# Half of the later feed-forward output pieces get their low part from an adding transfer, and the residual stands in DRAM while it is summed

## The chip, the cores and the metric

One core of a Trainium2 chip runs one decoder layer in float32. Five engines work side by side, each from its own list of instructions in order: TensorE (PE) multiplies, VectorE (DVE) and ScalarE (ACT) do elementwise work, GpSimd (POOL) does a little of that and issues transfers, and SyncE (SP) issues transfers. Instructions wait for each other by semaphores. The metric is the device time of one execution in microseconds (us).

## What is computed

A post-norm layer over 256 tokens of 2048 values: a feed-forward half step, a mixer (sparse attention beside a linear recurrence, with gates), and a second feed-forward half step, each added to its scaled input and normalised.

```python
def swiglu(h, w_in, w_out):
    a, b = jnp.split(h @ w_in, 2, axis=-1)
    return (jax.nn.silu(a) * b) @ w_out

h = layer_norm(DN_ALPHA * h + 0.5 * swiglu(h, ffn1_w_in, ffn1_w_out), ln1_g, ln1_b)
...                                     # mixer, merged
h = layer_norm(DN_ALPHA * h + merged @ w_out, ln2_g, ln2_b)
h = layer_norm(DN_ALPHA * h + 0.5 * swiglu(h, ffn2_w_in, ffn2_w_out), ln3_g, ln3_b)
```

D_FF is 5632, so each feed-forward reads an input matrix of 2048 x 11264 and an output matrix of 5632 x 2048. The change touches the two feed-forwards alone.

## The kernel before

**Three products for one.** PE multiplies in a rounded float32 form. To keep precision, each weight and each activation is split into a high part (the value rounded to that form) and a low part (the rest). A product is then three matmuls (`three`, L638 to L641): activation high by weight high, activation high by weight low, activation low by weight high.

**Pieces.** All weights come in the order of one list, `pieces`, each 128 x 1024 values (512 KB) or a part of a chunk of 128 x 2048 (1 MB). `Weights.load_to` has SP load piece i + 8 into a buffer `raw` (4 of these) or, for chunks, `rf` (2 of these) when PE's program is at piece i. `Weights.split_to` makes the two parts of piece i + 4: ScalarE copies with rounding into `wh` (L229), VectorE subtracts and writes `wl` (L230); there are 5 buffers of each. `unit` hands the parts to the matmuls.

**Chunks and plain pieces.** In a feed-forward the 22 column blocks of the input matrix follow each other. A block takes its weights as plain pieces (two products of 512 columns by two token tiles, 12 matmuls in all) or as chunks in a form with seven half-size products in place of eight (4 pieces named p1q3, p2, q5p7, q4p6; 12, 6, 12 and 12 matmuls of 256 columns), for which VectorE makes sums of weights first (L192, L196, L199). From block 6 on a block has four output pieces (`"o"` in its plan) and two plain input pieces beside three chunks (18 pieces), or four chunks and no plain input piece (20 pieces).

**The output product.** The 5632 rows of the output matrix are cut into six segments. While a segment's successor is being computed, output pieces of the segment run between its input pieces: `fill` multiplies one piece (12 matmuls of 512 columns) and after the last of four ScalarE takes the sums out of PSUM with a factor of 0.5 into `yd` (L1050), and POOL issues a transfer that adds `yd` to the residual `Y` in SBUF (L1051). Eight tiles `Y` of 128 x 512 hold the residual; they are among the 53 buffers of 128 x 512 that `U` hands out. The last segment has no successor: its pieces come after block 21, and its sums are added to `Y` by VectorE (`y_add`, L772), which then feeds the norm.

**What sets the order.** PE, SP and POOL run in the order in which the program writes their instructions. ScalarE's and VectorE's order is made by a scheduler from priorities and dependencies. Small tasks (norms, residual, gates) are stepped in the background once a piece.

## Time and profile before

| | |
|---|---|
| three runs | 2378.07, 2378.59, 2378.8 us (median 2378.59) |
| the profiled execution | 2379.03 us, its span 2377.3 us |
| PE busy | 2360.8 us (99%) |
| VectorE busy | 2211.1 us (93%) |
| ScalarE busy | 1491.2 us (63%) |
| DMA, loads by SP / transfers by POOL | 54.9% / 8.1% of 16 engines' span |
| clock granted to PE | 1.0 throughout |

How to read it: a row of a group gives line, engine, operation, tiles, shapes and count, then busy time and the mean of one in ns, then the idle time before it and what ended that. A row of waits gives who waited for whom, the sum in us, how often, and the longest. A row of the order of time gives start and duration in us. The span begins with the first instruction; the 1.7 us between span and time lie around it.

### The profile page before, as it was taken

To read this page: it belongs to the slowest core of one execution; us is meant where nothing else is said; L and a number is where in the kernel's file an instruction comes from. 1 tells how busy PE (TensorE), PEld (TensorE's weight loads), DVE (VectorE), ACT (ScalarE), POOL (GpSimd) and SP (SyncE) were. 2 spreads that over 40 slices of the span, in tenths; PEclk is the share of its full clock that TensorE was granted. 3 is DMA by queue.
4 is the path that set the end of the run, shared out by engine and by line. 5 is a ranking of instruction groups with operands and counts; after the bars stand their busy time and mean duration, and the time that the engine had idled before them with its cause. 6 is when DMAs were issued, how large, how long until landed. Compare 5 with 4: busy or idle time off the path is not lost.

```text
span 2377.3 us, 38831 instructions
## 1 busy us (share of the span) xinstructions
PE 2360.8 (99%) x14926; PEld 2106.8 (89%) x14926; DVE 2211.1 (93%) x3130; ACT 1491.2 (63%) x2040; POOL 123.8 (5%) x196
## 2 busy tenths in 40 slices
PE   9999999999999999999999999999999999999999
PEld 7898999989988888888999998888898899899997
DVE  7999999999999998789878889998999999999997
ACT  7666666666647555665578886555766666666663
POOL 0000000000000000001000001100000000000000
PEclk9999999999999999999999999999999999999999
DMA  8666666666566455537655558755676665676665
GB/s 302 192 226 211 223 213 221 218 218 213 189 219 222 177 186 172 191 132 269 208 185 183 182 181 292 263 199 173 208 231 213 222 212 187 230 230 210 215 214 177
DMA packets 123163, 499.69 MB, mean 210 GB/s; under 512 B 14272, under 2 KB 15552, under 8 KB 102112
## 3 DMA queue, kind: packets, MB, share of 16 engines
q1 hardware_dynamic: 104400, 453.03, 54.9%
q0 software_dynamic: 18576, 44.17, 8.1%
q8 instruction: 117, 1.92, 0.3%
q14 instruction: 70, 0.57, 0.1%
HBM read 465.68 MB, written 10.49 MB: 200 GB/s over the span
## 4 chain that ended last, share of the span: by engine, by line
PE 93%; DVE 4%; issue 1%; DMA 1%; ACT 0%; SPq 0%; POOL 0%; POOLq 0%; ACTq 0%; DVEq 0%
PE mm L641 20%; PE mm L639 20%; PE mm L640 20%; PE bp L640 6%; PE bp L641 6%; PE bp L639 6%; PE mm L1337 3%; PE mm L1339 3%; PE mm L1338 3%; DVE wl L230 2%; PE bp L1029 1%; DVE ws L192 0%; DMA x<-x_fm 0%; DMA raw<-f1a 0%; ACT wh L229 0%
## 5 line engine op out<-in xcount | busy, mean ns | idle before, releaser
L229 ACT ACTIVATE wh<-raw 128x1024 fp32r<-128x1024 f32 (+2 forms) x538 | 547.2, 1039 | 286.9 <-PE mm L641 162.8
L230 DVE TENSOR_TENSOR wl<-raw,wh 128x1024 fp32r<-128x1024 f32 (+2 forms) x538 | 631.3, 1191 | 96.8 <-ACT wh L229 94.6
L229 ACT ACTIVATE wh<-rf 128x1024 fp32r<-128x1024 f32 (+1 forms) x489 | 440.0, 915 | 312.9 <-PE mm L641 153.0
L230 DVE TENSOR_TENSOR wl<-rf,wh 128x1024 fp32r<-128x1024 f32 (+1 forms) x489 | 505.5, 1040 | 11.5 <-ACT wh L229 5.9
L639 PE MATMUL mm<-wh,hs 128*128 128x512 f32 (+1 forms) x884 | 317.0, 359 | 0.0
L641 PE MATMUL mm<-wh,hs 128*128 128x512 f32 (+1 forms) x884 | 311.2, 352 | 1.2 <-DVE hs L820 1.2
L640 PE MATMUL mm<-wl,hs 128*128 128x512 f32 (+1 forms) x884 | 310.8, 352 | 0.2 <-DVE wl L230 0.2
L641 PE MATMUL mm<-wh,g 128*128 128x512 f32 (+1 forms) x696 | 274.6, 394 | 0.0
L639 PE MATMUL mm<-wh,g 128*128 128x512 f32 (+1 forms) x696 | 274.4, 394 | 0.0
L640 PE MATMUL mm<-wl,g 128*128 128x512 f32 (+1 forms) x696 | 274.4, 394 | 0.0
L229 ACT ACTIVATE wh<-ws 128x1024 fp32r<-128x1024 f32 x163 | 173.1, 1062 | 144.1 <-PE mm L641 86.0
L639 PE MATMUL bp<-wh,sh 128*128 128x256 f32 x918 | 258.7, 282 | 0.0
L640 PE MATMUL bp<-wl,sh 128*128 128x256 f32 x918 | 256.4, 279 | 1.2 <-DVE wl L230 1.2
L641 PE MATMUL bp<-wh,sl 128*128 128x256 f32 x918 | 256.2, 279 | 0.0
L192 DVE TENSOR_TENSOR ws<-rf 128x1024 f32<-128x1024 f32 x163 | 198.4, 1217 | 9.5 <-DMA rf<-wrb 2.8
L230 DVE TENSOR_TENSOR wl<-ws,wh 128x1024 fp32r<-128x1024 f32 x163 | 198.1, 1215 | 1.3 <-ACT wh L229 1.0
L641 PEld LDWEIGHTS mm<-wh,hs 128*128 128x128 f32 x884 | 165.9, 188 | 27.6 <-DVE hs L820 2.6
L639 PEld LDWEIGHTS mm<-wh,hs 128*128 128x128 f32 x884 | 166.0, 188 | 24.3 <-issue 1.5
L640 PEld LDWEIGHTS mm<-wl,hs 128*128 128x128 f32 x884 | 166.1, 188 | 22.4 <-DVE wl L230 0.7
L1337 PE MATMUL mm<-hs,wh 128*128 128x256 f32 x640 | 179.8, 281 | 0.0
L1338 PE MATMUL mm<-hs,wh 128*128 128x256 f32 x640 | 179.8, 281 | 0.0
L1339 PE MATMUL mm<-hs,wl 128*128 128x256 f32 x640 | 179.8, 281 | 0.0
(353 smaller groups left out, 5276.3 us busy)
## 6 DMA issues: line engine op xcount, KB each, us to landing
rf<-f1a SPq DMA_DIRECT2D x64, 1024.0 KB, 5.4
rf<-f2a SPq DMA_DIRECT2D x64, 1024.0 KB, 5.7
raw<-f1o SPq DMA_DIRECT2D x88, 512.0 KB, 6.6
raw<-f2o SPq DMA_DIRECT2D x88, 512.0 KB, 6.6
raw<-wB SPq DMA_DIRECT2D x80, 512.0 KB, 4.0
raw<-wG SPq DMA_DIRECT2D x54, 512.0 KB, 4.3
raw<-f2a SPq DMA_DIRECT2D x48, 512.0 KB, 4.4
raw<-f1a SPq DMA_DIRECT2D x47, 512.0 KB, 5.4
```

The costliest lines, as they stand in the source:

```text
L192: v.tensor_tensor(t, b[:, 0:4:3], b[:, 1:2].to_broadcast([P, 2, 2, 256]), op=OP.add)
L229: nc.scalar.activation(hp, src, AF.Copy)
L230: self.last = nc.vector.tensor_tensor(lp, src, hp, op=OP.subtract)
L639: T.matmul(ps, xh, w[0], start=start, stop=False)
L640: T.matmul(ps, xh, w[1], start=False, stop=False)
L641: T.matmul(ps, xl, w[0], start=False, stop=stop)
L1029: T.transpose(ps[:, k * S + t * P:k * S + (t + 1) * P], z[:, t * 512 + k * P:t * 512 + (k + 1) * P], ident)
L1337: T.matmul(ps[:, :S], w[0], x[:, 0], start=first, stop=False)
L1338: T.matmul(ps[:, :S], w[0], x[:, 1], start=False, stop=False)
L1339: T.matmul(ps[:, :S], w[1], x[:, 0], start=False, stop=last)
```

## The change

Of the four output pieces of a segment and column block, the second and the fourth (`k` 2 and 6) in segments 1 to 4 are marked: two a block in blocks 6 to 21, 32 in each feed-forward.

A marked piece leaves the usual path. `far_to` loads its raw weights 14 pieces ahead (still 512 KB by SP, into `raw`), and ten pieces ahead ScalarE writes, for each half of 512 columns, the negated rounded weights into a tile `l` and the rounded weights into a tile `h` (both `wd`, from `U`); POOL issues a transfer that reads the same weights again from DRAM and adds them to `l`. What stands in `l` then is the weight minus its rounded form, the low part. VectorE's subtraction and the wide copy of such a piece are gone, and it uses no `wh` and `wl`.

The residual also leaves SBUF: at the start of each feed-forward's sums POOL stores the scaled residual to tiles `sums` in DRAM, the adding transfers of `fill` go there, and after block 21 eight transfers load it into fresh tiles `Y`.

```diff
@@ -59,6 +59,7 @@
 WS_BUFS = 1
 HL_BUFS = 5
 AHEAD = 4
+EARLY = 10
 LOADS = 4
 FORMS = ("p1q3", "p2", "q5p7", "q4p6")
 PIECE = 1024
@@ -151,6 +152,31 @@
         self.cur = -1
         self.limit = None
         self.off = 0
+        self.far = []
+        self.far_raw = {}
+        self.far_loaded = self.far_split = 0
+
+    def far_to(self, i):
+
+
+        nc = self.nc
+        while self.far_loaded < len(self.far) and self.far[self.far_loaded] <= i + LOADS:
+            k = self.far[self.far_loaded]
+            ap = self.pieces[k][0]
+            t = self.far_raw[k] = self.pool.tile([P, PIECE], F32, name=f"raw{k}", tag="raw", bufs=RAW_BUFS)
+            nc.sync.dma_start(t, ap)
+            self.far_loaded += 1
+        while self.far_split < len(self.far) and self.far[self.far_split] <= i:
+            k = self.far[self.far_split]
+            ap, t = self.pieces[k][0], self.far_raw.pop(k)
+            h, l = ([self.wide() for _ in range(2)] for _ in range(2))
+            for c in range(2):
+                nc.scalar.activation(l[c], t[:, c * 512:(c + 1) * 512], AF.Copy, scale=-1.0)
+                nc.gpsimd.dma_start(l[c], ap[:, c * 512:(c + 1) * 512], accum_op=OP.add)
+            for c in range(2):
+                nc.scalar.activation(h[c], t[:, c * 512:(c + 1) * 512], AF.Copy)
+            self.hl[k] = (h, l)
+            self.far_split += 1
 
     def key(self, i):
         ap, form = self.pieces[i]
@@ -165,7 +191,7 @@
         while self.loaded <= min(i, len(self.pieces) - 1):
             ap, form = self.pieces[self.loaded]
             k = self.key(self.loaded)
-            if k not in self.raw:
+            if k not in self.raw and self.loaded not in self.far:
                 n = ap.shape[1]
                 if form:
                     t = self.fast_pool.tile([P, 2 * PIECE], F32, name=f"rf{self.loaded}", tag="rf", bufs=RAWF_BUFS)
@@ -205,6 +231,9 @@
         nc = self.nc
         while self.split <= min(i, len(self.pieces) - 1):
             form = self.pieces[self.split][1]
+            if self.split in self.far:
+                self.split += 1
+                continue
             self.load_to(self.split)
             k = self.key(self.split)
             if self.split >= len(self.pieces) - WIDE:
@@ -238,6 +267,7 @@
             self.hl.pop(self.cur, None)
             self.cur += 1
             self.off = 0
+            self.far_to(self.cur + EARLY)
             self.load_to(self.cur + AHEAD + LOADS)
             self.split_to(self.limit or self.cur + AHEAD)
             self.on_piece()
@@ -245,7 +275,7 @@
         o = self.off
         self.off += n
         assert self.off <= self.size(self.cur)
-        if self.cur >= len(self.pieces) - WIDE:
+        if self.cur >= len(self.pieces) - WIDE or self.cur in self.far:
             return h[o // 512], l[o // 512]
         return h[:, o:o + n], l[:, o:o + n]
 
@@ -335,7 +365,7 @@
 
     bg = Background()
 
-    pieces = []
+    pieces, far = [], []
 
     def plain(aps):
         for ap in aps:
@@ -349,6 +379,8 @@
                 pieces.append((ap[:, k * 512:k * 512 + PIECE], None))
             elif f == "o":
                 g, nb, k = next(fills)
+                if k in (2, 6) and g:
+                    far.append(len(pieces))
                 k += 2 * SEGS[g][0]
                 pieces.append((fo[nb][:, k * 512:k * 512 + PIECE], None))
             else:
@@ -395,6 +427,7 @@
     ffn_pieces(f2a, f2o)
 
     W = Weights(nc, pool, pieces, bg.step)
+    W.far = far
     W.wide = lambda: U("wd", F32R)
     W.fast_pool = ctx.enter_context(tc.tile_pool(name="f1", bufs=1))
     lane, first_home, shared = [None], {}, ExitStack()
@@ -589,6 +622,8 @@
 
     Y = [[None] * 4 for _ in range(2)]
 
+    sums = [[[spill.tile([P, 512], F32, name=name("ya")) for _ in range(4)] for _ in range(2)] for _ in range(2)]
+
     def load_x():
         for _ in range(4):
             yield
@@ -600,6 +635,7 @@
         for nb in range(4):
             for t in range(2):
                 A.activation(Y[t][nb], Y[t][nb], AF.Copy, scale=ALPHA)
+                G.dma_start(sums[0][t][nb], Y[t][nb])
                 yield
 
     bg.add("y", load_x())
@@ -609,7 +645,7 @@
         G.dma_start(t, bass.AP(tensor=v.tensor, offset=v.offset + nb * 512, ap=[[0, P], [1, 512]]))
         return t
 
-    def residual(g, b, away=None):
+    def residual(g, b, away=None, to=None):
         for nb in range(4):
             gr, br = row(g, nb, "gr"), row(b, nb, "br")
             if away:
@@ -622,6 +658,8 @@
                 V.scalar_tensor_tensor(y, y, ALPHA, gr, op0=OP.mult, op1=OP.mult)
                 yield
                 V.scalar_tensor_tensor(y, br, ALPHA, y, op0=OP.mult, op1=OP.add)
+                if to:
+                    G.dma_start(to[t][nb], y)
                 yield
 
 
@@ -1035,6 +1073,7 @@
         g = [[None] * (2 * (b1 - b0)) for b0, b1 in SEGS]
         fills = iter(FILLS)
         open_ps = []
+        acc = sums[ln.last]
 
         def fill():
             s, nb, k0 = next(fills)
@@ -1048,7 +1087,7 @@
                 for t in range(2):
                     u = W.fast_pool.tile([P, 512], F32, name=name("yd"), tag="yd", bufs=2)
                     A.activation(u, open_ps[t], AF.Copy, scale=0.5)
-                    G.dma_start(Y[t][nb], u, accum_op=OP.add)
+                    G.dma_start(acc[t][nb], u, accum_op=OP.add)
 
         for s, (b0, b1) in enumerate(SEGS):
             for n in range(b0, b1):
@@ -1057,6 +1096,10 @@
                 with tc.high_priority():
                     next(task)
                 bg.add("gate", task)
+        for nb in range(4):
+            for t in range(2):
+                Y[t][nb] = U("y")
+                G.dma_start(Y[t][nb], acc[t][nb])
         new_stats((24, 30) if ln.last else (24, 24))
         if not ln.last:
             share("t")
@@ -1437,7 +1480,7 @@
 
 
     new_stats()
-    ln = InnerNorm("ln2_g", "ln2_b", FAST, lambda: bg.add("main", residual(ln2_g, ln2_b)))
+    ln = InnerNorm("ln2_g", "ln2_b", FAST, lambda: bg.add("main", residual(ln2_g, ln2_b, None, sums[1])))
     out_product(mg, ln, mg_forms)
     mg = mg_forms = None
     share("s")
```

Three places show how the rows move; numbers in `wh`, `wl`, `raw`, `rf` are those of the piece. They are taken at the end of block 9 of the first feed-forward: piece 152 is its successor's first output piece, 153 and 165 are marked ones of block 10, 143 is a marked one of block 9.

ScalarE, before, from the last chunk of block 9 to the output pieces of block 10:

```order
L229 ACTIVATE wh146_2959<-ws144_2932 128x1024
L229 ACTIVATE wh147_2976<-rf144_2855 128x1024
L1050 ACTIVATE yd168_2992<-mm159_2779 128x512
L1050 ACTIVATE yd169_2995<-mm160_2780 128x512
L229 ACTIVATE wh148_3000<-rf148_2928 128x1024
L229 ACTIVATE wh149_3020<-rf148_2928 128x512
L229 ACTIVATE wh150_3033<-ws148_3002 128x1024
L229 ACTIVATE wh151_3052<-rf148_2928 128x1024
L229 ACTIVATE wh152_3070<-raw152_2998 128x1024
L229 ACTIVATE wh153_3086<-raw153_3018 128x1024
L229 ACTIVATE wh154_3096<-raw154_3031 128x1024
L229 ACTIVATE wh155_3112<-raw155_3050 128x1024
```

ScalarE, now, from the same chunk on (`L174` writes the tile that the transfer adds to, `L177` the rounded weights):

```order
L258 ACTIVATE wh146_3033<-ws144_3006 128x1024
L174 ACTIVATE wd218_3052<-raw153_2988 128x512
L174 ACTIVATE wd219_3053<-raw153_2988 128x512
L177 ACTIVATE wd216_3050<-raw153_2988 128x512
L177 ACTIVATE wd217_3051<-raw153_2988 128x512
L258 ACTIVATE wh147_3060<-rf144_2931 128x1024
```

After four more rows of the same list:

```order
L258 ACTIVATE wh150_3115<-ws148_3086 128x1024
L258 ACTIVATE wh151_3134<-rf148_3002 128x1024
L258 ACTIVATE wh152_3152<-raw152_3082 128x1024
L258 ACTIVATE wh154_3174<-raw154_3113 128x1024
L258 ACTIVATE wh155_3192<-raw155_3132 128x1024
L174 ACTIVATE wd229_3279<-raw165_3190 128x512
L258 ACTIVATE wh156_3221<-rf156_3150 128x1024
```

The one copy of piece 153, which stood behind wh152, has become four and stands between wh146 and wh147; the first of piece 165 stands between wh155 and wh156. In the list of now the five `wh` before wh146 belong to the pieces 145, 144, 142, 141 and 140, since 143 is a marked one.

SP, before, the loads of the same pieces:

```order
L178 DMA rf139_2750<-f1a 128x2048
L178 DMA raw143_2835<-f1o 128x1024
L178 DMA rf144_2855<-f1a 128x2048
L178 DMA rf148_2928<-f1a 128x2048
L178 DMA raw152_2998<-f1o 128x1024
L178 DMA raw153_3018<-f1o 128x1024
L178 DMA raw154_3031<-f1o 128x1024
L178 DMA raw155_3050<-f1a 128x1024
L178 DMA rf156_3068<-f1a 128x2048
L178 DMA raw160_3139<-f1a 128x1024
L178 DMA rf161_3159<-f1a 128x2048
L178 DMA raw165_3231<-f1o 128x1024
```

SP, now:

```order
L167 DMA raw143_2794<-f1o 128x1024
L204 DMA rf139_2818<-f1a 128x2048
L204 DMA rf144_2931<-f1a 128x2048
L167 DMA raw153_2988<-f1o 128x1024
L204 DMA rf148_3002<-f1a 128x2048
L204 DMA raw152_3082<-f1o 128x1024
L204 DMA raw154_3113<-f1o 128x1024
L204 DMA raw155_3132<-f1a 128x1024
L204 DMA rf156_3150<-f1a 128x2048
L167 DMA raw165_3190<-f1o 128x1024
L204 DMA raw160_3219<-f1a 128x1024
L204 DMA rf161_3239<-f1a 128x2048
```

The loads of 143, 153 and 165 stand one or two rows further ahead; none is added.

POOL, before, in the same blocks, where it issues nothing but the adding transfers into `Y`:

```order
L1051 DMA y58_398<-yd156_2702 128x512
L1051 DMA y59_400<-yd157_2705 128x512
L1051 DMA y63_429<-yd168_2992 128x512
L1051 DMA y64_431<-yd169_2995 128x512
L1051 DMA y48_336<-yd180_3394 128x512
L1051 DMA y49_338<-yd181_3397 128x512
```

POOL, now:

```order
L175 DMA wd218_3052<-f1o 128x512
L175 DMA wd219_3053<-f1o 128x512
L1090 DMA ya29_206<-yd220_3076 128x512
L1090 DMA ya33_210<-yd221_3079 128x512
L175 DMA wd229_3279<-f1o 128x512
L175 DMA wd230_3280<-f1o 128x512
L175 DMA wd238_3400<-f1o 128x512
L175 DMA wd239_3401<-f1o 128x512
```

The two transfers of piece 153 (`wd218`, `wd219`) stand ahead of the pair that adds the sums ending with piece 143, those of piece 165 (`wd229`, `wd230`) behind it.

## The prediction

> **What bounds the kernel now.** I read the page's busy shares first, then the waits of TensorE over the whole span.
>
> ```profile
> PE 2360.8 (99%) x14926; PEld 2106.8 (89%) x14926; DVE 2211.1 (93%) x3130; ACT 1491.2 (63%) x2040; POOL 123.8 (5%) x196
> PEclk9999999999999999999999999999999999999999
> ```
>
> ```profile
> PE mm L639 <- ACT wh L229: 5.6, 1, 5.6
> ...
> PE bp L640 <- DVE wl L230: 1.2, 2, 0.7
> ...
> PE mm L640 <- DVE wl L230: 0.2, 1, 0.2
> ```
>
> These are the first, the fifth and the last of eight rows, which sum to 11.6 us of 2377. Half of it is the first weight at the start. VectorE, whose work the change removes, is the cause of 1.4 us. The change acts on blocks 6 to 21 of both feed-forwards, about 140 to 661 us and 1790 to 2313 us, so I asked for the waits there: for all engines in the first stretch (130 to 661), and for PE alone in the second (1800 to 2310), where one row is the whole answer.
>
> ```profile
> ACT wh L229 <- PE mm L641: 105.8, 95, 2.2
> ...
> DVE wl L230 <- ACT wh L229: 6.1, 10, 1.0
> ```
>
> ```profile
> PE bp L640 <- DVE wl L230: 0.5, 1, 0.5
> ```
>
> In the first stretch PE itself has no wait at all (its own answer is empty), and ScalarE's largest wait is for PE to give a buffer back (106 us, 95 times): the makers of operands run ahead of PE and are held by it. The busy times by stretch (columns: PE, PEld, DVE, ACT, POOL, then granted clock, DMA share, GB/s) say how close the race is.
>
> ```profile
> 940.00:990.00 50.00, 50.00 (x238) 41.36 (x238) 37.06 (x79) 27.52 (x56) 1.90 (x4) 1.00 0.56 176
> 301.00:396.00 95.00, 95.00 (x625) 86.22 (x623) 93.13 (x111) 60.76 (x75) 5.25 (x6) 1.00 0.66 216
> 1875.00:2050.00 175.00, 175.00 (x1142) 158.54 (x1142) 172.14 (x204) 111.10 (x135) 8.96 (x11) 1.00 0.65 211
> ```
>
> VectorE is 98% busy in the blocks (93.13/95), yet PE is never idle. A busy PE is not a PE at its peak, so I took its starts from the order of time.
>
> ```profile
> 302.57 0.28 PE L639 MATMUL mm<-wh,xs 128*128 128x256 f32 x1
> 302.69 0.28 PE L640 MATMUL mm<-wl,xs 128*128 128x256 f32 x1
> 303.97 0.39 PE L639 MATMUL mm<-wh,xs 128*128 128x512 f32 x1
> 304.20 0.39 PE L640 MATMUL mm<-wl,xs 128*128 128x512 f32 x1
> ```
>
> ```profile
> 941.91 0.39 PE L640 MATMUL mm<-wl,hs 128*128 128x512 f32 x1
> 942.15 0.40 PE L641 MATMUL mm<-wh,hs 128*128 128x512 f32 x1
> ```
>
> A product of 256 columns starts about 0.117 us after the one before, one of 512 about 0.233 us, and the second pair shows the same step where VectorE is only 74% busy (37.06/50) and the DMA at 0.56. In the blocks PE's own stream sets the time; VectorE only keeps up, with 2% to spare.
>
> **The change part by part.** The sum is made against the profiled execution's own time, 2379.03 us (span 2377.3 and 1.7 around it); the three runs' median is 2378.59, 0.44 below, and the forecast is moved by that.
>
> *Work taken from VectorE and given to ScalarE.* 64 pieces (32 in each feed-forward, two in each of 16 blocks) lose one wide subtraction and one wide copy, and get four half-wide copies.
>
> ```profile
> L230 DVE TENSOR_TENSOR wl<-raw,wh 128x1024 fp32r<-128x1024 f32 x516 | 620.1, 1219 | 93.9 <-ACT wh L229 91.7
> L229 ACT ACTIVATE wh<-raw 128x1024 fp32r<-128x1024 f32 x516 | 536.9, 1061 | 281.3 <-PE mm L641 162.8 <-PE mm L1338 44.3 <-issue 26.3
> L229 ACT ACTIVATE wh<-rf 128x512 fp32r<-128x512 f32 x163 | 101.9, 625 | 67.0 <-PE mm L641 65.3 <-PE bp L641 1.7
> ```
>
> VectorE: 64 x 1.22 = 78 us less, 2.4 us in each block. A block of 18 pieces has 126 products of 256 columns and 72 of 512, 14.7 + 16.8 = 31.5 us, so VectorE goes from 98 to about 90%. ScalarE: 64 x (4 x 0.625 - 1.06) = 92 us more, 2.9 us a block, from 64% (60.76/95) to about 73%. PE's products stay the same ones in the same order. What it can gain is its waits for VectorE there: 0.5 us by the row above, 0 as the lower bound, 1.4 us if every such wait of the span went. I take -0.2 us. The added 2.9 us of ScalarE cost nothing as long as PE's stream covers them: after it ScalarE still has 27% of a block, 8.5 us, and without that cover they would cost 92 us.
>
> *The adding transfers.* 128 transfers of 256 KB from DRAM, added into a half of a low part, issued by POOL. The trace has no such transfer; the nearest is the adding one from SBUF into the residual, the nearest from DRAM a plain load.
>
> ```profile
> L1051 POOL DMA_DIRECT2D y<-yd x80: 850/878/1215, 75.7 to 2313.9; - x80
> ...
> DMA to landing us min/median/max: 3.3/7.1/9.9
> ```
>
> ```profile
> q0 software_dynamic: 18576, 44.17, 8.1%
> ...
> rf<-f1a SPq DMA_DIRECT2D x64, 1024.0 KB, 5.4
> ...
> raw<-f1o SPq DMA_DIRECT2D x88, 512.0 KB, 6.6
> ...
> y<-ys POOLq DMA_DIRECT2D x8, 256.0 KB, 4.6
> ```
>
> Landing lies between 3.3 us and, if adding and fetching came one after the other, 9.9 + 6.6 = 16.5 us. I take 7.1, the adding row, since size and operation are its own. Against that stands the lead. In ScalarE's list of the change the low part of piece 153 stands behind wh146, which takes the buffer of piece 140 (five pieces back, as 143 has none there). Counting only from piece 142 on, PE still has to run 96 products of 256 columns (142, 144 to 151) and 24 of 512 (143, 152): 11.2 + 5.6 = 16.8 us. Two ScalarE copies (1.25) and two issues on POOL (1.75) leave 13.8 us for the landing; 7.1 is well inside, 9.9 too. Piece 165, the other kind, stands behind wh155 and has some 25 us. On POOL the transfers of 153 stand ahead of the residual's adding transfers, which wait for PE; those of 165 stand behind them, and are freed when piece 143 is done, more than 30 us ahead of use. So the cost is 0; its upper bound is in the rivals.
>
> *DMA load.* By the q0 row, 8.1% for 44.17 MB, 33.6 MB more take 6.2% of the span, all of it in the 1045 us of the two stretches: there 0.65 becomes about 0.79. Loads for the fast products get somewhat later; VectorE's 2.4 us a block cover that (second rival).
>
> *Raw pieces earlier on SP.* The 64 loads are the same ones, moved ahead of up to two others (the order on SP shows one or two places). The wide buffer is held for four pieces as before. Cost 0.
>
> *The residual in DRAM.* Eight stores behind the scaling at about 40 us, eight in the second residual, and eight loads at each end; the 80 adding transfers now have DRAM as their goal. At the first end:
>
> ```profile
> 659.57 1.75 POOL L1051 DMA_DIRECT2D y<-yd  x2 [25.38 <-ACT yd L1050]
> ```
>
> ```profile
> 688.58 1.28 DVE L772 SCALAR_TENSOR_TENSOR y<-mm,y 128x512 f32<-128x512 f32 x2
> ```
>
> From the last adding issue (661.3) to the first use of the residual (688.6) there are 27 us: a landing of at most 9.9, eight issues at 0.88 (7.0) and a landing of 4.6 take 21.5. The first use needs only the first two tiles. Cost 0, hidden by the last segment's products; if that cover were gone, up to 21.5 us at each of two ends. The eight buffers that the residual leaves are what two pieces in flight (four tiles each) need, so ScalarE finds no new wait for a buffer.
>
> Sum: 2379.03 - 0.2 + 0 + 0 + 0 + 0 = 2378.8, and 2378.4 on the scale of the median.
>
> **Rivals.**
>
> *VectorE was the hidden bound* (faster). For it: 98% busy, and PE's busy time is modelled. Then 2.4 us come back in each of 32 blocks, 77 us: 2301. Against it: PE's step is the same at 74% VectorE, and VectorE waits on ScalarE, ScalarE on PE. Chance 0.05. The Trainium skill, Perfetto Trace Analysis, Identifying the Most-Contended Engine, says just this of matmul busy time, that it is no measure of headroom, and points to the share of weight loading; PEld at 89% would by that rule leave PE up to 11% of room, in which VectorE's relief could show. The trace bears out that busy is modelled, but the steps leave no gap that a late operand made.
>
> *Loads for the fast products come late* (slower). VectorE works on one chunk while the next but one loads into the buffer just left.
>
> ```profile
> 498.04 1.22 DVE L192 TENSOR_TENSOR ws<-rf 128x1024 f32<-128x1024 f32 x1
> 499.17 1.22 DVE L230 TENSOR_TENSOR wl<-raw,wh 128x1024 fp32r<-128x1024 f32 x1
> ...
> 501.44 0.68 DVE L196 TENSOR_TENSOR rf<-ws,rf 128x512 f32<-128x512 f32 x1
> 502.05 0.68 DVE L230 TENSOR_TENSOR wl<-rf,wh 128x512 fp32r<-128x512 f32 x1
> ```
>
> Four wide steps of 1.13 and three of 0.61 make 6.4 us a chunk, against a landing of 5.4 and an issue of about 0.4. The removed subtractions also shorten the time between chunks. Each landing beyond 6.0 us makes VectorE wait; it has 0.6 + 2.4 = 3.0 us a block for three chunks, so it decides from a landing of 7.0 on. At 7.5 it is 3 x 1.5 - 3.0 = 1.5 us a block, 48 us: 2427. For it: the DMA's added share. Against: at 0.66 busy the loads land in 5.4, and operands are made up to four pieces ahead of PE. Chance 0.06.
>
> *The adding transfers land late* (slower). From 13.8 us on, PE waits in 32 pieces; at the bound of 16.5 that is 2.7 x 32 = 86 us: 2465. Against: the adding row's maximum is 9.9. Chance 0.03. The Trainium skill, SBUF — State Buffer, SBUF: two separate sides, has a rule for it: while VectorE holds the port it shares with GpSimd in a fast mode, GpSimd can't write descriptors, and a transfer of 0.62 us took 3.1. By that, as an estimate, 7.1 would become 35 us and the kernel some hundreds of us slower. The 80 adding transfers of this trace were issued beside a 98% busy VectorE and landed in 9.9 at most, so the row speaks against it.
>
> *The change does not put the transfers ahead*: POOL's queue could hold them behind a wait for PE. The order above excludes it for both kinds, and I give it nothing of its own.
>
> **How the numbers follow.** Forecast 0.86, VectorE bound 0.05, late loads 0.06, late transfers 0.03. Within 0.2% (4.8 us) counts as no change, about what runs of this kernel can tell. The forecast's own bounds are -1.4 and a few us of small waits at the ends; I take 2374 to 2385 as the range, which leaves out the two priced slower cases and the faster one, 0.14 in all. Faster 0.05, same 0.86, slower 0.09.
>
> **What would show it.** Right: VectorE near 90% and ScalarE near 73% in 301 to 396, DMA near 0.79, adding transfers landing within 10 us, PE's waits still about 12 us, its last segment starting at the same time. Wrong: a PE wait on a DMA into wd, VectorE waiting on rf for over 3 us a block, or PE's steps shorter than 0.233.

## The result, and the profile after

The changed kernel takes 2397.36 us (median of four runs, 2395.78 to 2399.16) against 2378.33 for the kernel before on the same chip: a ratio of 1.0080, with a 95% interval of 1.0063 to 1.0098, or 19 us slower. The profiled execution has a span of 2394.7 us.

The page of the changed kernel, its busy times and the shares of its chain of work that ended last:

```profile
PE 2363.3 (99%) x14926; PEld 2106.9 (88%) x14926; DVE 2143.1 (89%) x3066; ACT 1547.5 (65%) x2232; POOL 254.1 (11%) x356
...
PE 77%; DVE 10%; DMA 5%; issue 4%; ACT 3%; POOL 0%; SPq 0%; POOLq 0%; ACTq 0%; DVEq 0%
```

The same shares in the kernel before:

```profile
PE 93%; DVE 4%; issue 1%; DMA 1%; ACT 0%; SPq 0%; POOL 0%; POOLq 0%; ACTq 0%; DVEq 0%
```

VectorE is relieved as meant (2211 to 2143 us), PE has the same products, and yet the chain now leaves PE more often, for VectorE, the DMA and ScalarE. The waits of PE over the whole span tell where (engine, line, what was waited for, total us, times, longest); these are the first three of ten rows:

```profile
PE mm L677 <- DVE z L1055: 12.6, 12, 1.9
PE mm L677 <- ACT wh L258: 5.5, 1, 5.5
PE bp L678 <- DVE wl L259: 1.8, 3, 0.7
```

The first row is new. L1055 is the gate's last sum that reads the PSUM banks of a block; until it is done, the next block's products have no bank. A gap here is the time by which the start of one of PE's products comes later than the step of 0.117 or 0.233 us after the start of the one before. In the two feed-forwards 17 gaps of over 0.25 us hold 18.2 us, where the trace before has one, of 0.7 us. That is 17.5 us more, all of the loss (the spans differ by 17.4). The busy times by stretch, in the columns of the prediction, and after them the same third stretch of the kernel before:

```profile
301.00:396.00 95.00, 93.68 (x618) 84.84 (x616) 85.16 (x103) 64.55 (x91) 15.82 (x18) 1.00 0.83 249
1875.00:2050.00 175.00, 174.18 (x1157) 158.66 (x1156) 156.71 (x186) 122.24 (x168) 29.93 (x34) 1.00 0.84 247
661.00:700.00 39.00, 36.91 (x205) 31.22 (x204) 33.53 (x60) 20.21 (x27) 6.10 (x10) 1.00 0.88 294
```

```profile
661.00:700.00 39.00, 39.00 (x202) 32.53 (x201) 35.75 (x77) 19.63 (x25) 0.31 (x1) 1.00 0.67 197
```

VectorE has 10 us of 95 free, ScalarE 30, and PE loses 1.3. So it is no engine's work that lasts too long; somebody waits in the wrong place. The waits of all engines from 130 to 661 us, behind two rows of POOL:

```profile
...
ACT z L1056 <- DVE z L1055: 52.8, 17, 4.3
ACT wd L174 <- DMA raw<-f1o: 35.4, 15, 4.3
ACT wh L258 <- DVE rf L225: 27.7, 26, 2.2
DVE ws L218 <- DMA rf<-f1a: 24.4, 15, 2.5
ACT wh L258 <- PE mm L679: 23.8, 45, 1.7
```

Two engines now wait for loads: ScalarE for the raw load of a marked piece (L174 is the copy that makes its low part), 15 times, and VectorE at the first sum of a chunk (L218), 15 times (before: twice, 1.4 us). The last row says that ScalarE is held back by PE for 24 us, where it was 106. One gap in full: the chain of work that ends in PE's gap at 396 us (start, length, what).

```profile
376.32 1.24 DVE wl L259
...
377.58 0.33 SPq L204
...
377.95 11.55 DMA raw<-f1o
...
389.53 0.04 ACT wd L174
...
390.06 1.05 ACT wh L258
...
391.14 1.23 DVE wl L259
392.37 0.33 DVE z L1049
...
395.43 0.61 DVE z L1055
...
396.18 0.47 PE mm L677
```

And what SP (first five rows) and POOL issue ahead of it:

```profile
371.54 0.33 SPq L204 DMA_DIRECT2D rf<-f1a  x1
371.92 0.90 SPq L204 DMA_DIRECT2D raw<-f1o  x2
372.86 0.66 SPq L204 DMA_DIRECT2D raw<-f1a  x1
377.58 0.33 SPq L204 DMA_DIRECT2D rf<-f1a  x1
377.95 0.65 SPq L167 DMA_DIRECT2D raw<-f1o  x1
```

```profile
374.03 1.75 POOL L175 DMA_DIRECT2D wd<-f1o  x2 [18.07 <-ACT wd L174]
378.49 1.77 POOL L1090 DMA_DIRECT2D ya<-yd  x2 [2.70 <-ACT yd L1089]
```

It reads so: 2.5 MB of loads go out at 371 to 373 us, two adding transfers at 374, another 1 MB load at 377.6, when VectorE gives its buffer back, and behind it on SP the raw load of the marked piece (L167). That one lands after 11.5 us. ScalarE, which works in order, stands at the marked piece's copy for 3.9 us; the high part behind it, VectorE's subtraction after that and the gate's sums behind this come late, and PE waits 1.1 us for a bank. In both feed-forwards the second marked piece of nearly every block meets ScalarE so (68 us in 30 waits). Of the 18.2 us of gaps, 8.5 end a chain that has passed through the raw load of a marked piece within 22 us. Another 2.4, at 684 and 694 us, end one that has passed through the raw load of a plain output piece. Six gaps, 4.3 us, end chains that meet no such load in that time.

The other 3.1 us lie in two gaps before any marked piece of the second feed-forward. The chain that ends at 1735 us:

```profile
1726.87 0.61 DVE y L660
...
1727.77 0.54 POOL ya L662
1728.31 6.11 DMA gr<-ln_g
...
1734.44 0.69 DVE y L658
1735.13 0.34 DVE g L801
...
1735.52 0.50 PE mm L679
```

POOL issues the store of the residual (L662), which waits for VectorE's sum, and only behind it the load of the next rows for the normalisation (L645). These land 6 us later, VectorE waits for them at L658 (two waits, 4.1 us), and the operand that PE needs (L801) stands behind. The transfers themselves, from the DMA view:

```profile
q1 hardware_dynamic: 104400, 453.03, 53.6%
q0 software_dynamic: 39568, 86.12, 18.0%
...
rf<-f1a SPq DMA_DIRECT2D x64, 1024.0 KB, 6.6
...
wd<-f1o POOLq DMA_DIRECT2D x64, 256.0 KB, 7.2
```

The adding transfers land in 7.2 us, and PE never waits for one. The loads for the fast products have gone from 5.4 to 6.6 in the median; worked out from the single landings in 130 to 661 us, counted from the end of the issue, a quarter takes 7.2 or more (5.7 before) and one in twenty 8.5 or more (6.7).

### The profile page after: what moved, and what is told of

It reads as the page before. It is cut to its first block, busy times and chain, and to the rows that moved or that the text cites. A ratio compares the mean times of both kernels' runs of the same rounds, so it can differ in the third digit from the quotient of the medians.

```text
span 2394.7 us, 39215 instructions
## 1 busy us (share of the span) xinstructions
PE 2363.3 (99%) x14926; PEld 2106.9 (88%) x14926; DVE 2143.1 (89%) x3066; ACT 1547.5 (65%) x2232; POOL 254.1 (11%) x356
## 4 chain that ended last, share of the span: by engine, by line
PE 77%; DVE 10%; DMA 5%; issue 4%; ACT 3%; POOL 0%; SPq 0%; POOLq 0%; ACTq 0%; DVEq 0%
PE mm L677 17%; PE mm L679 17%; PE mm L678 16%; DVE wl L259 5%; PE bp L678 5%; PE bp L679 5%; PE bp L677 5%; PE mm L1380 3%; PE mm L1381 3%; PE mm L1382 3%; DMA raw<-f1o 2%; ACT wh L258 2%; DMA raw<-f2o 1%; DVE ws L218 1%; DVE rf L225 1%
## 5 line engine op out<-in xcount | busy, mean ns | idle before, releaser
L259 DVE TENSOR_TENSOR wl<-raw,wh 128x1024 fp32r<-128x1024 f32 (+1 forms) x474 | 557.0, 1187 | 128.6 <-ACT wh L258 126.4
L258 ACT ACTIVATE wh<-raw 128x1024 fp32r<-128x1024 f32 (+1 forms) x474 | 483.9, 1035 | 261.3 <-PE mm L679 135.3
L218 DVE TENSOR_TENSOR ws<-rf 128x1024 f32<-128x1024 f32 x163 | 198.6, 1218 | 53.5 <-DMA rf<-f1a 24.4
L679 PEld LDWEIGHTS mm<-wh,hs 128*128 128x128 f32 x884 | 165.9, 188 | 27.5 <-DVE hs L858 2.6
L678 PEld LDWEIGHTS bp<-wl,sh 128*128 128x128 f32 x918 | 172.7, 188 | 4.7 <-DVE wl L259 2.8
L677 PE MATMUL mm<-wh,g 128*128 128x512 f32 x440 | 173.9, 395 | 2.0 <-DVE z L1055 1.9
L679 PE MATMUL mm<-wh,g 128*128 128x512 f32 x440 | 173.6, 395 | 1.6 <-DVE g L801 1.6
```

The lines of the kernel that those rows point to most:

```text
L218: v.tensor_tensor(t, b[:, 0:4:3], b[:, 1:2].to_broadcast([P, 2, 2, 256]), op=OP.add)
L258: nc.scalar.activation(hp, src, AF.Copy)
L259: self.last = nc.vector.tensor_tensor(lp, src, hp, op=OP.subtract)
L677: T.matmul(ps, xh, w[0], start=start, stop=False)
L678: T.matmul(ps, xh, w[1], start=False, stop=False)
L679: T.matmul(ps, xl, w[0], start=False, stop=stop)
```

## The experiments

All times are medians beside runs of the kernel before on the same chip (2378.8 to 2379.3 us). "Residual" stands for the residual's way through DRAM, "marks" for the marked pieces. The runs without adding transfers (no_add, e19_noadd) leave the low parts of the marked pieces unfinished.

| run | what is left or changed | us | ratio, 95% interval |
|---|---|---|---|
| res_only | residual, no marks | 2386.2 | 1.0031 (1.0019 to 1.0043) |
| no_add | marks without adding transfers, residual | 2383.9 | 1.0021 (1.0012 to 1.0029) |
| raw7 | marked raw loads three pieces earlier | 2399.0 | 1.0087 (1.0073 to 1.0100) |
| rows | residual's stores behind the next rows' loads | 2394.1 | 1.0060 (1.0048 to 1.0073) |
| one2 | first mark of a block alone, residual | 2390.2 | 1.0046 (1.0033 to 1.0058) |
| one6 | second mark alone, residual | 2385.1 | 1.0023 (1.0014 to 1.0032) |
| early8 | both, begun 8 ahead | 2424.9 | 1.0190 (1.0176 to 1.0204) |
| early12 | both, begun 12 ahead | 2406.6 | 1.0117 (1.0103 to 1.0131) |
| one2e15 | one2 begun 15 ahead | 2402.7 | 1.0103 (1.0089 to 1.0117) |
| one6e19 | one6 begun 19 ahead | 2401.9 | 1.0091 (1.0078 to 1.0105) |
| far_sb | both marks, residual in SBUF | 2386.5 | 1.0037 (1.0023 to 1.0050) |
| one6sb | second mark, residual in SBUF | 2378.0 | 0.9995 (0.9987 to 1.0004) |
| ballast | kernel before plus the transfers | 2379.8 | 1.0002 (0.9994 to 1.0011) |
| e19_noadd | one6e19 without its transfers | 2383.2 | 1.0016 (1.0007 to 1.0025) |
| sbfour | one6sb, ten four-chunk blocks | 2381.0 | 1.0010 (1.0001 to 1.0019) |
| four0 | kernel before, ten four-chunk blocks | 2403.7 | 1.0100 (1.0086 to 1.0114) |
| rf3 | a third buffer for fast products' loads | 2394.9 | 1.0067 (1.0054 to 1.0080) |
| vec_ballast | marks split by VectorE, transfers as ballast | 2387.3 | 1.0036 (1.0024 to 1.0048) |

**First set: what in the change costs.**

```diff
 res_only
-                if k in (2, 6) and g:
+                if False and k in (2, 6) and g:
 no_add
-                nc.gpsimd.dma_start(l[c], ap[:, c * 512:(c + 1) * 512], accum_op=OP.add)
 raw7
-RAW_BUFS = 4          U_BUFS = 53
+RAW_BUFS = 5          U_BUFS = 51
-        while self.far_loaded < len(self.far) and self.far[self.far_loaded] <= i + LOADS:
+        while self.far_loaded < len(self.far) and self.far[self.far_loaded] <= i + LOADS + 3:
 rows (for nb = 3: after the loop)
             gr, br = row(g, nb, "gr"), row(b, nb, "br")
+            if to and nb:
+                for t in range(2):
+                    G.dma_start(to[t][nb - 1], Y[t][nb - 1])
...
-                if to:
-                    G.dma_start(to[t][nb], y)
```

> The residual goes through DRAM as in the change, but no piece is marked: no adding transfer for a low part, no early raw load. Theory A (the second marked piece of a block gets its raw load late, because the load stands on SP behind a load for a fast product that waits for VectorE; ScalarE waits in order, and the gate's sums come late): the loss of the marked pieces goes, the 3.1 us that the two gaps at 1733 and 1749 us show stay: 2381 us. Theory B (the bytes of the adding transfers make all loads late): the same 2381. Theory C (the residual through DRAM is the loss): 2394 to 2397. Theory C in its small form (rows for the normalisation queued behind the stores on POOL): PE gaps at about 1720 to 1750 us stay, and nothing else.

> The change without the 128 adding transfers of the marked pieces (so their low part holds minus the raw values, a part of the computation that is left out); the early raw loads and all four ScalarE copies stay. Theory B: DMA back at about 0.66 in the blocks, loads for the fast products back at 5.4 us, loss gone but for the 3 us of the residual: 2380 to 2383. Theory A: the raw loads of the second marked pieces still stand behind the loads for the fast products, and only their landing gets shorter (11 to perhaps 7 us): some of the 10.9 us stays, 2385 to 2392. Theory D (the order of VectorE's list and ScalarE's added work alone): 2394 to 2397.

> The change with the raw loads of the marked pieces asked for three pieces earlier (one load for a fast product earlier on SP), with a fifth raw buffer to hold them, paid for by two of the 53 half-wide buffers. All transfers and all work stay. Theory A: ScalarE's waits for the raw loads (68 us) go, and with them the 10.9 us of TensorE gaps that end a chain from such a load: 2384 to 2388. Theory B: the bytes are the same, no change: 2395 to 2399. Theory D: no change.

> The change with the stores of the second residual issued after the next pair of rows for the normalisation is asked for on POOL, not before. Theory C in its small form: the two gaps at 1733 and 1749 us go, 3.1 us: 2394. Theories A, B and D: these gaps are no part of them; nothing else moves.

The residual alone costs 7.4 us, more than the two gaps I had found. In its trace the gaps over 0.25 us hold 4.3 us at 1728 to 1789 us, 0.7 at 687 (the end of the first feed-forward) and 0.3 at 157. With the stores behind the rows' loads (rows) both gaps at 1733 and 1749 us are gone, and the median is 3.3 us below the change's; the intervals of the two ratios overlap, so the size rests on the trace. Without the adding transfers the loss of the blocks is gone, and with it Theory D: the window of no_add,

```profile
301.00:396.00 95.00, 95.00 (x626) 86.46 (x625) 87.11 (x105) 66.66 (x93) 5.21 (x6) 1.00 0.65 217
```

has PE whole again, with ScalarE's added copies and VectorE's shorter list in place and the DMA back at 0.65. Theory A, the place of the raw load on SP, falls as I had put it: with these loads three pieces earlier ScalarE's waits for them in the first feed-forward halve (35.4 to 17.7 us), but the time stays. The earlier loads make other groups (one load for the fast products in twenty now takes 11.6 us instead of 8.5), and PE waits for high and low parts instead of for a bank. As half of ScalarE's waits are still there, this run alone does not clear them.

**Second set: bytes or place.** The marks one at a time, and both begun earlier or later.

```diff
 one2 / one6
-                if k in (2, 6) and g:
+                if k == 2 and g:          # one6: k == 6
 early8 / early12
-EARLY = 10
+EARLY = 8                             # early12: 12
```

> Only the first of the two marked pieces of a block stays marked (32 pieces in all, half of the added bytes); the second is split by VectorE as before. Residual through DRAM as in the change. The loss of the change beyond the run without adding transfers is 2397.4 - 2383.9 = 13.5 us. If the bytes as such decide (a mean share of the DMA), half of them cost about half or less: 2387 to 2391, and the same for the second piece alone. If what decides is where the transfers fall among the loads (the first piece's transfers are issued while four loads of 2.5 MB are under way, the second's between two such groups), this piece carries most: 2391 to 2396.

> Only the second marked piece of a block stays marked. Mean share: 2387 to 2391, as with the first alone. Place among the loads: its transfers fall into a light stretch of the DMA, so 2384 to 2387, near the run without adding transfers (2383.9).

> The change with its marked pieces begun eight pieces ahead instead of ten (their raw load, copies and adding transfers all some 3.5 us later against the other loads); the same bytes. Mean share: 2396 to 2399 again. Place among the loads: another time, by more than 3 us, since another group of loads is met. The lead shrinks from 13.8 to about 10 us, still above the 7.1 us of landing.

> The same with twelve pieces ahead (some 3.5 us earlier). Mean share: 2396 to 2399. Place among the loads: another time, by more than 3 us.

The two marks move the same bytes, at the same share of the DMA, but differ by 5 us. First one2, then one6, in 301 to 396:

```profile
301.00:396.00 95.00, 94.28 (x621) 85.59 (x620) 90.22 (x108) 63.30 (x83) 10.56 (x12) 1.00 0.74 233
```

```profile
301.00:396.00 95.00, 95.00 (x625) 86.31 (x624) 90.60 (x108) 63.24 (x84) 10.64 (x12) 1.00 0.75 233
```

and the waits for the loads, in the same order:

```profile
DVE ws L218 <- DMA rf<-f1a: 17.5, 14, 2.4
DVE ws L218 <- DMA rf<-f2a: 17.3, 15, 2.6
```

```profile
ACT wd L174 <- DMA raw<-f1o: 23.3, 14, 2.9
ACT wd L174 <- DMA raw<-f2o: 4.8, 7, 1.7
```

one2 costs 4 us over the residual's 7.4 without one wait at a marked piece's copy: it is the loads for the fast products that are waited for, by VectorE (35 us in 29 waits) and by ScalarE's copies of their high parts (9 us in 8); one6 costs nothing over it, though ScalarE waits 28 us: at most 2.9 us at a time, and its raw loads land in 5.0 and 3.8 us in the median of the two feed-forwards. So a mean share doesn't decide. early12 says the same, 9 us more than the change with the same bytes. early8 brings something else: the 27.5 us that it is above the change are mostly PE waiting for the adding transfers themselves,

```profile
PE mm L678 <- DMA wd<-f1o: 12.0, 8, 2.3
PE mm L678 <- DMA wd<-f2o: 10.7, 8, 2.1
```

which POOL, in its order, issues here behind the residual's adding transfers, whose operand waits for PE. For place against share it tells nothing.

**Third set: the place foretold, and the two halves of the change apart.**

```diff
 one2e15 / one6e19
-EARLY = 10
+EARLY = 15                            # one6e19: 19
 far_sb (one6sb the same, with k == 6)
-                G.dma_start(sums[0][t][nb], Y[t][nb])
...
-                    G.dma_start(acc[t][nb], u, accum_op=OP.add)
+                    G.dma_start(Y[t][nb], u, accum_op=OP.add)
...
-                Y[t][nb] = U("y")
-                G.dma_start(Y[t][nb], acc[t][nb])
```

> As the run with only the first marked piece (2390.2 us), but begun fifteen pieces ahead instead of ten. Its transfers were issued at 308.0, 340.1 and 372.6 us, 2 to 6 us behind the start of a group of loads; some 9 us earlier they fall into the stretches where the DMA stands at 0.5 and less (about 294 to 302, 329 to 334, 358 to 368). The same bytes. If the place among the loads decides: near the run with the second piece alone, 2384 to 2387. If the mean share decides, or this piece is dear for another reason: 2389 to 2392.

> The other way round: only the second marked piece (2385.1 us with ten ahead, its transfers at 293, 324, 351 and 389 us in light stretches), begun nineteen pieces ahead, some 16 us earlier, so that its transfers meet the groups of loads that begin at about 301, 334 and 369 us. The same bytes. Place among the loads: dearer by 3 to 8 us, 2388 to 2393. Mean share: 2384 to 2387 as before.

> Both marked pieces, but the residual stays in SBUF through the sums as in the kernel before (no stores, no reloads, the 80 adding transfers end in SBUF), with the same 53 half-wide buffers. If the two losses add: 2397.4 less the 7.4 us of the run with the residual alone, about 2390. If the buffers that the residual holds are too few for two pieces in flight, ScalarE waits for a buffer and the time is above 2397.

> Only the second marked piece, and the residual in SBUF. If the residual through DRAM is nearly all that is left of the loss with this piece alone (6 of 6 us): 2378 to 2380, no change against the kernel before, as the prediction had it for the work moved off VectorE.

one6e19 went the way foretold, and further (17 us dearer than with ten ahead; again no wait at a marked piece's copy, but waits for the loads for the fast products, 55 us in 31 of VectorE and 25 us in 12 of ScalarE). one2e15 went against it: 12 us dearer where I had it cheaper. In its trace the transfers were issued at 296, 322, 361 and 392 us, not in the light stretches I had read off the other run: the raw loads of the marks move with them, and a new group (1 MB and twice 0.5 MB at 292.6 to 293.7) stood just ahead of them. A place read from one trace doesn't hold when the move itself shifts the loads. far_sb and one6sb answer cleanly: with the residual in SBUF both marks cost 7.5 us, the second alone nothing at all. The two losses of the change, 7.4 and 7.5, make 15 of its 19; together they cost 4 us more.

**Fourth set: the transfers alone, the rest alone, and what the relief is worth.**

```diff
 ballast (residual in SBUF, nothing marked)
+                self.spare = [self.pool.tile([P, 512], F32, ...) for c in range(4)]
...
+                t = self.spare[2 * (self.far_split % 2) + c]
+                nc.scalar.activation(t[:, :8], self.hl[self.cur][0][:, :8], AF.Copy)
+                nc.gpsimd.dma_start(t, ap[:, c * 512:(c + 1) * 512], accum_op=OP.add)
 e19_noadd (one6e19)
-                nc.gpsimd.dma_start(l[c], ap[:, c * 512:(c + 1) * 512], accum_op=OP.add)
 sbfour (one6sb) / four0 (the kernel before)
-FOUR = (9, 12, 15, 18, 21)
+FOUR = (7, 9, 10, 12, 13, 15, 16, 18, 19, 21)
```

> The kernel before (residual in SBUF, nothing marked, all low parts by VectorE, no raw load moved) with 128 adding transfers of 256 KB from DRAM added as ballast: each goes into one of four spare tiles that nobody reads, paced by a copy of 8 columns on ScalarE at the place where the change copies its low part. Nothing of the kernel's own work waits for them. If the DMA time that these transfers take is the cause by itself: loads for the fast products late, VectorE (which has no 2.4 us a block to spare here) waits, 2390 to 2410. If the loss needs what else a marked piece does (ScalarE's copies, raw loads asked for early, the shorter list of VectorE): 2378 to 2382.

> As the run with the second piece alone, begun nineteen pieces ahead (2401.9 us), without its 64 adding transfers (low part left out, so it holds minus the raw values). If those transfers at that place are the cause: 2384 to 2387, the time of the residual alone. If the earlier raw load or the longer held buffers are: 2396 to 2402.

> A use of the relief: only the second piece marked, residual in SBUF (2378.0 us), and ten instead of five of the 16 blocks with a fourth chunk of fast products in place of two plain pieces. A block of 20 pieces has 4 x 4.9 = 19.6 us of fast products against 14.7 + 5.6: TensorE saves 0.7 us a block, 10 blocks, 7 us. VectorE pays about 4.0 us for such a block and has 1.22 x 16 = 19.5 us a feed-forward from the marked pieces, 5 blocks' worth. If VectorE's time decides: 2371 to 2374. If the loads (a late landing by the added transfers) decide: 2378 or above.

> The control: the kernel before with the same ten blocks of four chunks and no marked piece. VectorE, 98% busy before, gets 5 x 4 = 20 us more a feed-forward than it has: if VectorE's time decides, slower than before, some 2390 to 2410; if PE's work alone, 2371 to 2374 as with the marked piece.

The ballast was the surprise. Its DMA is as full as the change's, and its slowest loads land as late (of those for the fast products one in twenty in 9.6 us or more, raw loads in 10.4; 8.5 and 9.9 in the change), though fewer of them are slow (a quarter of those for the fast products in 6.3 or more, 7.2 in the change). But PE loses nothing:

```profile
301.00:396.00 95.00, 95.00 (x624) 86.22 (x623) 93.59 (x111) 61.63 (x87) 15.83 (x18) 1.00 0.83 250
```

```profile
ACT wh L250 <- PE mm L667: 95.7, 89, 2.5
...
DVE ws L213 <- DMA rf<-f1a: 2.9, 2, 1.6
```

The rest alone (e19_noadd) costs nothing over the residual either: 2383.2, as no_add. So it takes both, and one count shows how they meet. From the issue of a load for the fast products to VectorE's first sum of it, a quarter of the loads of 130 to 661 us have 8.0 us or less in the kernel before and in the ballast run, 5.9 in no_add, 6.1 in the change. Loads that land in 7.0 to 8.5 us fit the first and not the second.

That the ballast's transfers come at other times than the change's could still be the whole difference. The traces can be set against each other: each load's landing in one run, against the time that the same load has until VectorE's first sum in another. The result is an estimate of how long VectorE would wait in 130 to 661 us. With the times of the kernel before, the ballast's landings give 1.6 us of waits and the change's 3.6. With the times of no_add, which itself has no such wait, they give 21.6 and 24.6 (the change has 24.4). So at VectorE it is late landings and shortened lists together, and the ballast's landings would have been late enough.

For raw loads: a plain one lies landed for 8.6 us (median) before ScalarE reads it in the kernel before, 8.2 in the ballast run. In the change the first marked one of a block still lies for 7.4 us, but the second for none: ScalarE is mostly there first. In no_add ScalarE waits for marked raw loads too, but 9.9 us in 9 waits instead of 68 in 30. A plain piece's copies wait for a buffer that PE has to give back (the 95.7 us above), and the load lands meanwhile. A marked piece's copies find their buffers free (in the change they have no wait but the one for the load), so ScalarE comes to them as soon as its list allows, ahead of the load.

VectorE's relief has a worth where its time decides: with ten blocks of four chunks the kernel goes to 2403.7 without a mark and to 2381.0 with one. But PE's 7 us don't appear, so no version was found that beats the kernel before: one6sb is level with it.

**Fifth set: at VectorE or at ScalarE.**

```diff
 rf3
-U_BUFS = 53            RAWF_BUFS = 2
+U_BUFS = 49            RAWF_BUFS = 3
 vec_ballast (far_sb)
-                nc.scalar.activation(l[c], t[:, c * 512:(c + 1) * 512], AF.Copy, scale=-1.0)
-                nc.gpsimd.dma_start(l[c], ap[:, c * 512:(c + 1) * 512], accum_op=OP.add)
+                nc.scalar.activation(self.spare[c][:, :8], h[c][:, :8], AF.Copy)
+                nc.gpsimd.dma_start(self.spare[c], ap[:, c * 512:(c + 1) * 512], accum_op=OP.add)
+                nc.vector.tensor_tensor(l[c], t[:, c * 512:(c + 1) * 512], h[c], op=OP.subtract)
```

> The change with a third buffer for the fast products' loads (paid for by four of the 53 half-wide buffers), so that each of these loads is asked for one chunk earlier. All transfers and all work stay. In the change a quarter of these loads has less than 6.1 us from issue to its first sum (8.0 before), and lands in 6.0 to 8.5. If the late landing meets the shortened lead at VectorE's first sum: VectorE's waits for these loads (47 us) go, and the loss falls to what the residual in DRAM costs, 2384 to 2388. If ScalarE's waits for the raw loads (68 us) carry it: 2393 to 2398.

> Residual in SBUF. Both marked pieces of a block begin ten ahead with their early raw load, but VectorE makes their low part (two half-wide subtractions, 1.4 us, where the kernel before has one wide of 1.2); the 128 adding transfers go as ballast into two spare tiles that nobody reads. Against the run with the marked pieces and the residual in SBUF (2386.5 us): the same bytes, early loads and early copies, but VectorE's list is as long as before, and its first sum of a chunk stands behind the plain pieces' subtractions again. If the shortened lead at VectorE is needed for the loss: 2378 to 2382, like the ballast alone. If ScalarE's in-order wait for the early raw loads is enough: 2385 to 2390.

rf3 took VectorE's waits away and little of the time:

```profile
ACT wd L174 <- DMA raw<-f1o: 42.4, 15, 4.4
ACT wd L174 <- DMA raw<-f2o: 38.2, 14, 4.4
...
DVE ws L218 <- DMA rf<-f1a: 0.7, 1, 0.7
```

It still costs 8.5 us more than res_only. Six of its gaps, 5.2 us, end a chain that passed through a marked piece's raw load and ScalarE's copy of it. So ScalarE's wait is enough for a loss, as the late loads for the fast products were in one2 and one6e19. How much it alone costs in the change this run doesn't say: it has four half-wide buffers fewer, and other groups of loads. vec_ballast doesn't tell: its waits for loads are mostly gone (28 us of 89 in far_sb), but PE waits for low parts there,

```profile
PE bp L678 <- DVE wl L263: 8.0, 13, 1.0
```

behind the marks' subtractions, which stand early in VectorE's list. It is slow for a reason of its own.

## Why the prediction was wrong

Three terms that the prediction put at 0 were not 0: the DMA load and the raw pieces' place on SP, together 7.5 us with the residual left in SBUF (far_sb), and the residual in DRAM, 7.4 us (res_only). Some 4 us more come when all are there. In the prediction's order:

- *What bounds the kernel* held: PE's own stream, with VectorE only keeping up. Less work on VectorE brought nothing where the loads were in time (one6sb 2378.0; no_add, with VectorE at 87.1 of 95 and PE whole), so the rival "VectorE was the hidden bound" is out.
- *Work moved to ScalarE, cost nothing* held for the work (no_add) and missed the order. I costed the four copies by their length and asked whether ScalarE has time; it has (its busy time rose by 56 us, not 92, to 68% in 301 to 396; VectorE's fell by 68, not 78). I did not ask what ScalarE does when it comes to them before their load: it stands, with the next chunk's high parts behind it.
- *The adding transfers* landed in 7.2 and 7.1 us (median), as taken. The slowest took 12.2, more than the 10 I had set as a sign but inside the 13.8 of lead, and PE waited for none; early8 shows the failure that the order on POOL kept away at ten ahead. The third rival is out, and with it the long stall of its rule: what VectorE mostly runs here is TENSOR_TENSOR, which, by the Trainium skill, SBUF — State Buffer, Who interferes with whom, has no two-port mode. The trace agrees, with 7.2 us beside a VectorE that is 90% busy (85.16 of 95 us).
- *DMA load, covered by VectorE's 2.4 us* is the step that failed first: it was put at 0, and VectorE's waits for these loads went to 47 us. The share was mis-sized a little (0.83 for 0.79), but the cover was wrong in kind. I compared a median landing with an average spare time. The loads come in groups, and the tail decides; and VectorE's spare 10 us in 95 lie at other places than its waits, while the gate's sums that free PE's banks stand right behind them.
- *Raw pieces earlier on SP, cost 0* failed: a load asked for four pieces ahead is as early as before only if the one who reads it is held as before. For the second marked piece of a block it went from 8.6 us of slack to none, and ScalarE waited 68 us.
- *The residual in DRAM, cost 0* failed: 7.4 us. I looked at the reload at the end of a feed-forward, where one end shows 0.7 us in res_only, and not at what stands behind the new stores on POOL. 3.1 us of it are the rows' loads; the remaining 4 I could only partly place (about 1 us more at 1731 and 1789, 1 at 687 and 157; the profiled execution of res_only is itself 1.3 us faster than its median).
- The nearest rival was *loads for the fast products come late*. It had the mechanism, even that the removed subtractions shorten the time between chunks, but decided by a landing of 7.0 us, which the medians (6.6 and 6.0) never reached, and its price of 48 us was too high since most loads still land in time. ScalarE's wait was in no rival.

What stays open: the 4 us that the two losses cost together beyond their sum; the gap of 2.1 us at 684 us, behind a plain raw load beside the residual's reload (DMA 0.88 there, 0.67 before), which far_sb does not have; why one2e15 came out as dear as it did, with no run without its transfers; and a version with marked pieces copied only after their load is surely there, which was not tried.

## What to carry to other kernels

An operation that is moved ahead loses the waits that used to hold it back, so ask of each of its inputs whether they were in time only thanks to these waits, and of each in-order engine what stands behind it. When transfers are added to a DMA that is 0.65 busy, compare the tail of the landings, group by group, with the shortest time from issue to first use, not a median with a mean. Before a store is put into a queue, read what loads follow it there: they inherit its wait.

## What was not expected of the hardware

- Per byte, an adding transfer from DRAM takes twice the DMA time of a load. The rows of the ballast run:

```profile
q1 hardware_dynamic: 104400, 453.03, 54.3%
q0 software_dynamic: 37008, 77.73, 16.1%
```

  Against the kernel before, 33.6 MB more took 16.1% of 2380.3 less 8.1% of 2377.3 us, 191 us of all 16 engines: 5.7 us a MB. The loads of q1 take 54.3% of 2380.3 us for 453 MB, 2.9 us a MB. The Trainium skill, Collectives: The Full Stack, The bandwidth ceiling: the fold count and why AG ≠ RS ≠ AR, has a rule for sums made in a ring collective: the add itself is free but needs two source reads, so the rate is half. The ratio of 2.0 is of that size; but the loads here have rows of 4 and 8 KB and the adding transfers of 2 KB, and no run parts the two. In no_add, 8.4 MB of plain stores and reloads with rows of 2 KB took 9.6% of 2380.6 less 193 us, 36 us or 4.3 us a MB, if the 80 adding transfers of the sums, which end in DRAM there, cost what they cost into SBUF. So much of the ratio may be the rows' length.
- What transfers of one queue cost through the loads of another does not follow from the mean share: at 0.73 to 0.75 the same bytes cost 0, 4 and 16 us over the residual's run (one6, one2, one6e19; without its adding transfers one6e19 costs nothing over it). The Trainium skill, DMA: Bandwidth & Descriptors, Issuing engines are not separate DMA queues, says that transfers of all issuing engines run on the same 16 DMA engines and interleave; the ballast run agrees, with the raw loads' slowest twentieth going from 7.8 to 10.4 us by transfers that POOL issued.
- A DMA at 0.83 with loads for the fast products of up to 10 us, and raw loads of up to 12, cost this kernel nothing (ballast) as long as its lists were in the old order.
